# The low part of the MLP weights: an accumulating DMA in place of a subtraction on VectorE or GpSimd

## The chip, the cores and the metric

The kernel runs on one core of one Trainium2 chip. The metric is the device time of one execution in microseconds (us). In the profile PE is the tensor engine (PEld its weight loads), DVE is VectorE, ACT is ScalarE, POOL is GpSimd, and SP is the engine that only issues transfers.

## What is computed

One inference step of a two-layer decoder on 576 tokens (512 prompt tokens and 64 sample tokens). Each layer has a mixing part (retention, window attention, memory attention, gates, an output projection `w_out` and a LayerNorm) and an MLP part. The change touches the weights of the MLP alone:

```python
    x = layer_norm(ALPHA * x + merged @ w_out, ln1_g, ln1_b)
    h = jnp.square(jax.nn.relu(x @ w_up))                      # 1024 -> 4096
    return layer_norm(ALPHA * x + h @ w_down, ln2_g, ln2_b)    # 4096 -> 1024
```

All of it is float32. The kernel gets float32 accuracy out of the faster float32r matmul by keeping every operand in two parts: `hi`, the value rounded to float32r, and `lo`, what the rounding left (`lo = value - hi`). A product is then three matmuls into one PSUM bank: hi x hi, lo x hi, hi x lo.

## The kernel before

**Weights.** All projection weights are cut into units of 128 partitions x 1024 numbers (512 KB), 154 units a layer, in the order in which they are used. The last 64 units of a layer are the MLP's: four blocks `c`, each of 8 units of `w_up` (`("up", c, m)`) and 8 of `w_down` (`("dn", c, m)`). The eight units ahead of them are those of `w_out` (`("wo", m)`). For each unit `fetch()` has SP load the raw weights into a tile of the pool `A` (25 tiles), and `split()` makes `hi` and `lo` from it. In `split_into()` the rounding goes to ACT or DVE and the subtraction to DVE or POOL, whichever a clock kept while the program is written (`Clock`) takes to be free first (`soonest`, `rounded`, `pick`). Of the 128 MLP units, 75 are rounded on ACT and 53 on DVE; 120 are subtracted on DVE and 8 on POOL.

**Tokens.** They are two groups, A with 256 tokens and B with 320. One step (`mstep`) multiplies one unit with one group: 24 matmuls into one of three PSUM banks named `pg`, after which ACT or DVE evacuates the bank. A step needs a free bank, so it waits for the evacuation of three steps before.

**Order.** Normally a unit is used for A and then for B (`both`). Around the LayerNorms the order is skewed: the eight `wo` units run for A, then the same eight for B; then the eight `up` units of block 0 run for A, then for B; the last `dn` block is done like this too. So A's LayerNorm (`norm_ev`, generators `shift`, `half`, `last`) is worked off on DVE, ACT and POOL while PE does B's `wo` steps, and B's LayerNorm while PE does A's `up` steps. In these runs a new unit is due every A step, in the rest of the MLP every A and B step together.

**When a unit is split.** `tick()` runs after every few matmuls. It splits the next unit if that one is due within `LOOK` = 24 us of the plan, is no more than `cap` units ahead of the last one finished, and ACT is about to be idle (or it is due within 4 us). Instructions on an engine run in the order in which they were written, so a split that stands ahead of other work on ACT, DVE or POOL holds that work up.

The diff touches `split()` alone:

Of the kernel before, what the change touches and what calls it, by code (L numbers as in the profile page):

```python
# [11 lines left out]
AF = mybir.ActivationFunctionType  # L12
ALU = mybir.AluOpType
# [5 lines left out]
D = 1024  # L19
# [43 lines left out]
def unit_order():  # L63
    o = [("mk", m) for m in range(4)] + [("mv", i) for i in range(4)]
    for p in range(4):
        o += [("rk", p), ("rq", p), ("rv", p, 0), ("rv", p, 1), ("rg", 2 * p), ("rg", 2 * p + 1)]
    o += [("sv", 0), ("sk", 0)] + [("sq", m) for m in range(4)]
    for m in range(8):
        o += [("gr", m), ("br", m)]
    o += [("mq", m) for m in range(4)]  # L70
    for g, b in (("gs", "bs"), ("gm", "bm")):
        for i in range(4):
            o += [(g, 2 * i), (g, 2 * i + 1), (b, i)]
    o += [("wo", m) for m in range(8)]
    for c in range(4):
        o += [("up", c, m) for m in range(8)] + [("dn", c, m) for m in range(8)]
    return o
# [160 lines left out]


class Clock:  # L240
    """An estimate, kept while the program is written, of when each engine gets to an instruction. It only decides in
    which order independent work is put into the engines' queues."""
    HOP = 0.15

    def __init__(self):
# [98 lines left out]


class Pe(tuple):
    """What the tensor engine reads next, in a generator's yield."""


class Filler:  # L350
# [65 lines left out]
class Builder:  # L416
# [67 lines left out]
        return self.cst[:rows, a:b]  # L484

    def soonest(self, choices, *ins):
        """The engine of the (name, cost) pairs that is likely to end first with an operation on ins."""
        c = self.clock
        t = max([c.now] + [c.ready((i,)) for i in ins])
        return getattr(self.nc, min(choices, key=lambda x: max(c.te[x[0]], t) + x[1])[0])  # L490
# [18 lines left out]
    def fetch(self, u):  # L509
        self.raw[u] = self.tile([P, 8, P], tag="A")  # L510
        self.nc.sync.dma_start(self.raw[u], self.I["wall"][u])
        if u >= XFROM:
            next(self.between, lambda: None)()

    def split(self, u):
        raw = self.raw.pop(u)
        k = unit_order()[u % UNITS]
        if k[0] == "wo":
            b = True
        elif k[0] in ("up", "dn"):  # L520
            b = u % 2 == 0
        else:
            b = k[0] in ("gr", "br") and u % 4 == 0
        tl = "B" if b else "A"
        hi = self.tile([P, 8, P], F32R)
        lo = self.tile([P, 8, P], F32R, tag=tl)
        self.split_into(hi, lo, raw, True)
        self.w[u] = (hi, lo)

    def tick(self):  # L530
# [67 lines left out]
        return r  # L598

    def load_x(self, X):  # L600
        """The loads of x and of the constants, which fetch() starts between those of the first weights; yields then
        the splits of x."""
        sync = self.nc.sync
        raws = []

        def part(g, j):
            raw = self.tile([P, 4, NG[g]], tag=g)
            sync.dma_start(raw, self.I["xT"][:, 4 * j:4 * j + 4, OFF[g]:OFF[g] + NG[g]])
            raws.append((g, raw))

        def const(*names):
            for k in names:
                sync.dma_start(getattr(self, k), self.I[k])
        todo = [lambda: part("A", 0), lambda: part("A", 1), lambda: const("cst"), lambda: part("B", 0),
                lambda: part("B", 1), lambda: const("rope", "par")]

        def split():
            for i in range(4):
                while i >= len(raws):
                    yield 0.5  # L620
                g, raw = raws[i]
                yield (raw,)
                X.setdefault(g, {"h": [], "l": []})
                h = self.tile([P, 4, NG[g]], F32R, tag=g)
                lo = self.tile([P, 4, NG[g]], F32R, tag=g)
                self.split_into(h, lo, raw, True)
                X[g]["h"].append(h)
                X[g]["l"].append(lo)
        self.between = iter(todo)
        return split()  # L630

    def load_mem(self, M):
# [61 lines left out]
            V.scalar_tensor_tensor(out, a, 1.5, out, ALU.add, ALU.mult)  # L694

    def norm_ev(self, g, y, l, gi, eps, out, scale=None, bias=1.0):
        """Evacuation of the eight chunks of one token group that ends in LayerNorm. The sums of y - c and (y - c)^2
        grow chunk by chunk; c is the mean of the first two chunks, so that E[(y-c)^2] is at most four times the variance."""
        nc = self.nc
        V, S, T, G = nc.vector, nc.scalar, nc.tensor, nc.gpsimd  # L700
        n = NG[g]
# [3 lines left out]
            return self.par[:, l, gi + q:gi + q + 1], self.par[:, l, gi + 8 + q:gi + 9 + q]  # L705

        def mean(ps, src):
            """As a generator: the mean of src over the features. 1/D is exact in float32r, the two parts of src add up
            to src."""
            if out is None and g == "A":  # L710
                yield Pe((src,))
                T.matmul(ps, lhsT=self.ones.bitcast(F32), rhs=src, start=True, stop=True)
                return
            yield (src,)
            hi, lo = (self.tt()[:, :n].bitcast(F32R) for _ in range(2))
            self.split_into(hi, lo, src, True)
            yield Pe((lo,))
            for i, x in enumerate((hi, lo)):
                T.matmul(ps, lhsT=self.ones, rhs=x, start=(i == 0), stop=(i == 1))

        def shift():
            pm = self.bank("a")[:, :n]
            yield from mean(pm, st["acc"])
            yield (pm,)
            st["c"] = self.u(n)
            V.tensor_scalar(st["c"], pm, 4.0, None, ALU.mult)
            cb = st["c"].unsqueeze(1).to_broadcast([P, 4, n])
            self.pick(y[1], st["c"], bias=bias).tensor_tensor(y[1], y[1], cb, ALU.subtract)
# [12 lines left out]
        def last():  # L741
            p1, p2 = self.bank("a")[:, :n], self.bank("a")[:, :n]
            yield from mean(p1, st["acc"])
            yield from mean(p2, st["s2"])
            yield (p1,)
            t = self.tile([P, 320], tag="ln", bufs=2)[:, :n]
# [310 lines left out]
            yield Pe((t,))  # L1057

    def hi_lo(self, hi, lo, src):
        """As a generator: the two parts of src, in float32r."""  # L1060
        self.nc.scalar.copy(hi, src)
        yield (hi,)
        e = self.nc.vector if src.space == PSUM else self.pick(src, hi)
        e.tensor_tensor(lo, src, hi.bitcast(F32), ALU.subtract)
# [624 lines left out]
        return X2  # L1689

    def lazy(self, step, gen):
        """The step, once the generator gen() that computes its operand has run to its end."""
        def fn():
            self.fill.finish(gen())
            step[1]()
        return (step[0], fn, step[2])
# [76 lines left out]
```

## Time and profile before

| | before |
|---|---|
| time, median of 2 runs | 2206.39 us (2205.45 to 2207.34) |
| span of the profiled execution | 2203.7 us |
| PE busy | 2155.0 us (98%) |
| DVE busy | 1251.4 us (57%) |
| ACT busy | 678.1 us (31%) |
| POOL busy | 324.3 us (15%) |
| DMA, mean over the span | 99 GB/s |

Busy shares are means over stages with different limits. The stage in which an engine's time counts is the one in which another engine waits for it; the idle time in front of an instruction, and what ended it, show that. Almost all lines of code carry the number L331, since one helper records every operation, so instructions are told apart by the tiles they write and read (`B<-B,pg` writes a B tile and reads a B tile and a `pg` bank).

### The profile page before, as it was taken

Reading aid. Unit: us, or ns where it says so; the run is one execution under the profiler, and the core shown is the slowest. Engines: PE = TensorE matmul, PEld = TensorE weight load, DVE = VectorE, ACT = ScalarE, POOL = GpSimd, SP = SyncE. Lnnn points to the kernel's source line nnn. Section 1 sums busy time; section 2 is a strip of 40 time slices with the busy share of each in tenths; the row PEclk is TensorE's granted clock in tenths of the full one; section 3 lists DMA queues with packets and bytes.
Section 4 is the critical chain, followed back from the end, with each engine's and each line's share of the span. In section 5 each row is a group of like instructions: output and inputs, shape, how many; then the busy total and the mean of one; then the engine's idle time right before and its main releaser. Section 6 shows DMA issues by size and latency. Waiting matters only on the chain. (4 is left out here: it accounts for less than half of the span.)

```text
span 2203.7 us, 38686 instructions
## 1 busy us (share of the span) xinstructions
PE 2155.0 (98%) x16466; PEld 2095.4 (95%) x16466; DVE 1251.4 (57%) x2334; ACT 678.1 (31%) x1400; POOL 324.3 (15%) x283
## 2 busy tenths in 40 slices
PE   9999999999999999999999999999999999999996
PEld 8999999999998999999989998999999899999996
DVE  6666855456677434343876568554565864343346
ACT  3222234232135141405342221442321450504042
POOL 0222300011032000000432223000210420000003
PEclk9999999999999999999999999999999999999998
DMA  8222212333331222223252222122444222222211
GB/s 305 81 86 93 82 49 77 107 136 143 120 126 63 91 87 77 86 96 96 84 175 83 84 83 91 59 76 97 144 154 149 86 68 86 81 91 77 87 49 43
DMA packets 66732, 217.41 MB, mean 99 GB/s; under 512 B 7232, under 2 KB 16960, under 8 KB 66496
## 3 DMA queue, kind: packets, MB, share of 16 engines
q1 hardware_dynamic: 50944, 168.27, 22.8%
q0 software_dynamic: 10528, 38.80, 5.0%
q10 hardware_dynamic: 5088, 7.87, 1.1%
q8 instruction: 129, 2.11, 0.4%
q14 instruction: 43, 0.35, 0.1%
HBM read 200.89 MB, written 15.99 MB: 98 GB/s over the span
## 5 line engine op out<-in xcount | busy, mean ns | idle before, releaser
L331 PE MATMUL pg<-B,A 128*128 128x320 f32 x5920 | 1030.2, 311 | 13.5 <-DVE B L331 11.9
L331 PE MATMUL pg<-A,A 128*128 128x256 f32 (+1 forms) x6720 | 962.1, 286 | 12.5 <-DVE A L331 5.4
L331 PEld LDWEIGHTS pg<-B,A 128*128 128x128 f32 x5920 | 907.9, 189 | 20.1 <-DVE B L331 14.4
L331 PEld LDWEIGHTS pg<-A,A 128*128 128x128 f32 x6720 | 892.4, 192 | 29.2 <-issue 11.7
L331 DVE TENSOR_TENSOR A<-A,A 128x1024 fp32r<-128x1024 f32 (+4 forms) x234 | 270.0, 1161 | 65.3 <-ACT A L331 60.9
L331 ACT CAST A<-A 128x1024 fp32r<-128x1024 f32 (+4 forms) x263 | 238.0, 925 | 94.9 <-DVE A L331 73.1
L331 PE MATMUL pg<-A,B 128*128 128x256 f32 x1088 | 248.0, 283 | 0.0
L331 PE MATMUL pg<-B,B 128*128 128x320 f32 x704 | 219.4, 312 | 0.0
L331 ACT ACTIVATE u<-pg 128x320 f32<-128x320 f32 (+1 forms) x128 | 52.6, 411 | 477.0 <-PE pg L331 476.8
L331 POOL TENSOR_TENSOR A<-A,A 128x1024 fp32r<-128x1024 f32 (+2 forms) x43 | 92.8, 2162 | 679.5 <-ACT A L331 621.5
L331 PEld LDWEIGHTS pg<-A,B 128*128 128x128 f32 x1088 | 181.8, 192 | 0.0
L331 DVE TENSOR_TENSOR B<-u,B 128x320 fp32r<-128x320 f32 x80 | 39.3, 492 | 190.8 <-ACT B L331 190.8
L331 ACT ACTIVATE t<-pg 128x256 f32<-128x256 f32 (+1 forms) x128 | 52.6, 411 | 292.3 <-PE pg L331 292.1
L331 PEld LDWEIGHTS pg<-B,B 128*128 128x128 f32 x704 | 134.1, 191 | 0.0
L331 POOL TENSOR_TENSOR B<-A,A 128x1024 fp32r<-128x1024 f32 x13 | 35.4, 2720 | 555.1 <-ACT A L331 497.2
L331 DVE TENSOR_TENSOR B<-A,A 128x1024 fp32r<-128x1024 f32 x77 | 97.2, 1263 | 17.5 <-ACT A L331 16.2
L331 DVE CAST A<-A 128x1024 fp32r<-128x1024 f32 (+1 forms) x112 | 85.2, 760 | 7.4 <-DMA A<-d 7.3
L331 DVE TENSOR_TENSOR B<-B,pg 128x320 f32<-128x320 f32 x56 | 27.0, 484 | 106.8 <-PE pg L331 106.7
L331 DVE TENSOR_TENSOR B<-B,u 128x256 f32<-128x256 f32 (+3 forms) x84 | 74.5, 895 | 2.4
L331 POOL TENSOR_TENSOR A<-A,cst 128x512 fp32r<-128x512 f32 x32 | 43.7, 1394 | 152.7 <-ACT A L331 152.7
L331 DVE SCALAR_TENSOR_TENSOR B<-t,pg 128x320 f32<-128x320 f32 (+1 forms) x48 | 22.3, 464 | 72.0 <-ACT t L331 52.9
L331 DVE SCALAR_TENSOR_TENSOR u<-t,pg 128x256 f32<-128x256 f32 x64 | 28.8, 450 | 57.4 <-PE pg L331 57.3
(200 smaller groups left out, 1623.1 us busy)
## 6 DMA issues: line engine op xcount, KB each, us to landing
A<-in_wall SPq DMA_DIRECT2D x305, 512.0 KB, 3.3
A<-in_mck POOLq DMA_DIRECT2D x16, 512.0 KB, 4.2
A<-in_mcv POOLq DMA_DIRECT2D x16, 512.0 KB, 5.9
A<-in_s POOLq DMA_DIRECT2D x8, 512.0 KB, 4.4
out_state_s<-A POOLq DMA_DIRECT2D x8, 512.0 KB, 3.2
d<-A POOLq DMA_DIRECT2D x6, 512.0 KB, 7.7
A<-d ACTq DMA_DIRECT2D x6, 512.0 KB, 5.5
rc<-in_rc POOLq DMA_DIRECT2D x8, 256.0 KB, 3.0
```

Of the source, the lines that this page charges most:

```text
L331: r = f(*a, **kw)
```

## The change

For `up` and `dn` units the rounding goes to ACT always; ACT then writes the rounded weight with its sign turned into `lo` (a second pass over the raw weights, rounded in the same way), and a DMA issued by POOL adds the raw weights to it in SBUF. All other units, and all activations, are split as before. The diff also takes comments out, which changes nothing.

```diff
@@ def split(self, u):
         tl = "B" if b else "A"
         hi = self.tile([P, 8, P], F32R)
         lo = self.tile([P, 8, P], F32R, tag=tl)
-        self.split_into(hi, lo, raw, True)
+        if k[0] in ("up", "dn"):
+            self.nc.scalar.copy(hi, raw)
+            self.nc.scalar.activation(lo, raw, AF.Copy, scale=-1.0)
+            self.nc.gpsimd.dma_start(lo, raw, accum_op=ALU.add)
+        else:
+            self.split_into(hi, lo, raw, True)
         self.w[u] = (hi, lo)
```

Per MLP unit this leaves two ACT passes over 128x1024 and one 512 KB transfer from SBUF to SBUF on POOL's queue, in place of a rounding and a subtraction. The DMA waits for ACT's second pass; PE waits for the DMA; the tile of raw weights comes free when the DMA has landed.

The order of instructions shifts at two places. The first is on DVE, in the eight `wo` steps for group B, while A's LayerNorm is worked off. `B919` and `B920` are the two halves of B's accumulated row `y`, `pg` the banks that PE waits for, `par` the LayerNorm's gains, `A917` and `A918` A's `y`. Before, from the evacuation of the fourth B step to that of the fifth:

```order
L331 TENSOR_TENSOR A1017_7219<-A1005_7152,A1016_7218 128x1024
L331 SCALAR_TENSOR_TENSOR B919_6560<-B919_6560,pg1013_7188 128x320
L331 TENSOR_SCALAR A917_6556<-A917_6556,par8_85 128x256 x2
L331 TENSOR_TENSOR A1003_7145<-A917_6556,A1001_7143 128x512
L331 TENSOR_SCALAR A917_6556<-A917_6556,par8_85 128x256 x2
L331 TENSOR_TENSOR A1003_7145<-A917_6556,A1001_7143 128x512
L331 TENSOR_SCALAR A918_6557<-A918_6557,par8_85 128x256 x2
L331 TENSOR_TENSOR A1004_7146<-A918_6557,A1002_7144 128x512
L331 TENSOR_SCALAR A918_6557<-A918_6557,par8_85 128x256 x2
L331 TENSOR_TENSOR A1004_7146<-A918_6557,A1002_7144 128x512
L331 TENSOR_TENSOR B920_6561<-B920_6561,pg1018_7240 128x320
```

With the change, the same stretch:

```order
L331 SCALAR_TENSOR_TENSOR B919_6560<-B919_6560,pg1013_7191 128x320
L331 TENSOR_SCALAR A917_6556<-A917_6556,par8_85 128x256 x2
L331 TENSOR_TENSOR A1001_7138<-A917_6556,A999_7136 128x512
L331 TENSOR_SCALAR A917_6556<-A917_6556,par8_85 128x256 x2
L331 TENSOR_TENSOR A1001_7138<-A917_6556,A999_7136 128x512
L331 TENSOR_TENSOR B920_6561<-B920_6561,pg1018_7244 128x320
```

The subtraction of a weight (first row of before) is gone, and the evacuation of the fifth step stands behind two of the four pairs that finish A's LayerNorm, no longer behind all four.

The second place is on ACT, in the `up` steps of block 0 for group A. `u` rows are the evacuations of a step (squared ReLU and its rounding), `ln` rows belong to B's LayerNorm. Before:

```order
L331 CAST A1053_7479<-A1019_7259 128x1024
L331 CAST A1056_7491<-A1045_7435 128x1024
L331 ACTIVATE u1058_7501<-pg1051_7463 128x256
L331 ACTIVATE u1058_7501<-u1058_7501 128x256
L331 CAST A1032_7380<-u1058_7501 128x256
L331 ACTIVATE ln1059_7507<-pa1030_7378 128x320
L331 ACTIVATE ln1063_7525<-u1061_7522 128x320
L331 ACTIVATE ln1063_7525<-ln1063_7525 128x320
L331 ACTIVATE u1064_7542<-pg1060_7509 128x256
```

With the change, from the same evacuation of the third step on:

```order
L331 ACTIVATE u1056_7506<-pg1052_7470 128x256
L331 ACTIVATE u1056_7506<-u1056_7506 128x256
L331 CAST A1032_7385<-u1056_7506 128x256
L331 ACTIVATE ln1059_7513<-u1057_7510 128x320
L331 ACTIVATE ln1059_7513<-ln1059_7513 128x320
L331 CAST A1067_7552<-A1043_7416 128x1024
L331 ACTIVATE A1068_7553<-A1043_7416 128x1024
L331 ACTIVATE u1069_7563<-pg1060_7517 128x256
```

The rounding of the last of the eight `up` units (`A1056` before, `A1067` with the change) stood ahead of the third evacuation; it now stands behind it and behind the two `ln` rows, with the new negating pass at its heels.

## Rows read from the trace of the kernel before

**Rows 1.** Page, part 1: busy time, share of the span, instructions.

```profile
PE 2155.0 (98%) x16466; PEld 2095.4 (95%) x16466; DVE 1251.4 (57%) x2334; ACT 678.1 (31%) x1400; POOL 324.3 (15%) x283
```

**Rows 2.** Stretches: us, busy of PE, PEld, DVE, ACT, POOL, clock, DMA share, GB/s.

```profile
660.00:680.00 20.00, 14.49 (x81) 13.96 (x82) 18.84 (x27) 5.93 (x11) 9.92 (x8) 0.83 0.16 54
680.00:700.00 20.00, 20.00 (x168) 20.00 (x167) 16.79 (x22) 15.29 (x33) 4.98 (x7) 1.00 0.09 27
740.00:1040.00 300.00, 300.00 (x2252) 300.00 (x2251) 112.97 (x163) 83.51 (x167) 0.00 (x0) 1.00 0.26 85
...
1750.00:1770.00 20.00, 14.44 (x81) 13.66 (x80) 18.83 (x28) 7.91 (x14) 8.43 (x7) 0.84 0.21 73
```

**Rows 3.** Timeline of PE: start us, length us, what, [idle before <- releaser].

```profile
660.67 0.41 PE L331 MATMUL pg<-B,A 128*128 128x320 f32 x1 [0.67 <-DVE B L331]
673.09 0.63 PE L331 MATMUL pg<-B,A 128*128 128x320 f32 x1 [4.74 <-DVE B L331]
...
1765.43 0.64 PE L331 MATMUL pg<-B,A 128*128 128x320 f32 x1 [4.77 <-DVE B L331]
```

**Rows 4.** Timeline of PEld: the 24 weight loads of one undisturbed B step.

```profile
843.08 3.54 PEld L331 LDWEIGHTS pg<-B,A 128*128 128x128 f32 x24
```

**Rows 5.** Timeline of DVE in layer 0's `wo` steps for B.

```profile
645.96 0.69 DVE L331 CAST A<-A 128x1024 fp32r<-128x1024 f32 x1
646.68 1.22 DVE L331 TENSOR_TENSOR B<-A,A 128x1024 fp32r<-128x1024 f32 x1
...
650.21 2.65 DVE L331 TENSOR_TENSOR ln<-ln 128x256 f32<-128x256 f32 x1
...
653.91 2.52 DVE L331 SCALAR_TENSOR_TENSOR u<-ln,ln 128x256 f32<-128x256 f32 x1
...
662.89 1.21 DVE L331 TENSOR_TENSOR A<-A,A 128x1024 fp32r<-128x1024 f32 x1
...
665.75 2.77 DVE L331 TENSOR_TENSOR A<-A,A 128x512 fp32r<-128x512 f32 x1
668.45 0.72 DVE L331 TENSOR_SCALAR A<-A,par 128x256 f32<-128x256 f32 x2
669.20 0.69 DVE L331 TENSOR_TENSOR A<-A,A 128x512 fp32r<-128x512 f32 x1
...
672.56 0.48 DVE L331 TENSOR_TENSOR B<-B,pg 128x320 f32<-128x320 f32 x1
```

**Rows 6.** Timeline of POOL in the same stretch: subtractions for weights.

```profile
650.16 2.42 POOL L331 TENSOR_TENSOR A<-A,A 128x1024 fp32r<-128x1024 f32 x1 [4.76 <-ACT A L331]
...
653.55 2.59 POOL L331 TENSOR_TENSOR B<-A,A 128x1024 fp32r<-128x1024 f32 x1
...
665.52 2.45 POOL L331 TENSOR_TENSOR B<-A,A 128x1024 fp32r<-128x1024 f32 x1
```

**Rows 7.** Groups by shape, 740 to 1040 us: busy us, mean ns, idle before.

```profile
L331 DVE TENSOR_TENSOR A<-A,A 128x1024 fp32r<-128x1024 f32 x24 | 29.4, 1226 | 6.0 <-ACT A L331 5.6
L331 DVE TENSOR_TENSOR B<-A,A 128x1024 fp32r<-128x1024 f32 x23 | 28.2, 1226 | 5.5 <-ACT A L331 5.1
L331 ACT CAST A<-A 128x1024 fp32r<-128x1024 f32 x23 | 24.1, 1049 | 0.0
L331 DVE TENSOR_TENSOR A<-u,A 128x256 fp32r<-128x256 f32 x24 | 10.2, 425 | 16.8 <-ACT A L331 16.8
```

**Rows 8.** Page, parts 3 and 6: POOL's queue q0; KB, us from issue to landing.

```profile
q0 software_dynamic: 10528, 38.80, 5.0%
...
A<-in_wall SPq DMA_DIRECT2D x305, 512.0 KB, 3.3
A<-in_mck POOLq DMA_DIRECT2D x16, 512.0 KB, 4.2
...
d<-A POOLq DMA_DIRECT2D x6, 512.0 KB, 7.7
```

**Rows 9.** Timeline of POOL around 1093 us: two issues of 512 KB each.

```profile
1093.42 1.60 POOL L331 DMA_DIRECT2D d<-A  x2
```

**Rows 10.** Groups by shape on POOL, whole span: an issue of 512 KB.

```profile
L331 POOL DMA_DIRECT2D A<-in_mck x16 | 8.7, 546 | 133.4 <-PE pg L331 105.7 <-DVE A L331 26.1 <-PE pa L331 1.6
```

**Rows 11.** Timeline of ACT and PE at the end of A's `up` steps.

```profile
690.80 0.47 ACT L331 ACTIVATE ln<-ln 128x320 f32<-128x320 f32 x1
...
699.56 3.16 PE L331 MATMUL pg<-A,A 128*128 128x256 f32 x25
```

More of the change, by code (lines that the diff above doesn't have):

```diff
@@ L346 @@
 class Pe(tuple):
+    pass
 class Filler:
```

## The prediction

> **What bounds the kernel now.** I read the busy times first, then the stretches, then the waits in the few stretches that are not full. PE is busy for 2155.0 of 2203.7 us [rows 1], so 48.7 us of idle time is all that could come back at PE's present pace. The stretches say where: from 740 to 1040 us, which is the MLP's blocks after the first `up` run, PE is busy for 300.00 of 300.00 us at full clock while DVE works for 113 us, ACT for 84 and POOL not at all [rows 2]. The work that the change takes from DVE there keeps nobody waiting. The stretch 660 to 680 us is different: PE is busy for 14.49 us of 20, its granted clock is 0.83 of full on the mean, and DVE works for 18.84 us [rows 2]. That is where B's `wo` steps run over A's LayerNorm. PE idles for 4.74 us until DVE has evacuated a bank, and for 0.67 us a little ahead of that [rows 3]; layer 1 shows the same hole, 4.77 us [rows 3], 0.84 of the clock and 81 matmuls in both [rows 2]. So DVE sets the time there, and MLP weights are split on it in that very stretch.
>
> **What the hole costs.** An undisturbed B step issues 24 matmuls in 3.54 us [rows 4], 0.1475 us each. The 81 matmuls of the 20 us [rows 2] should take 11.9 us; 8.1 us are lost, some 5.5 of them idle and the rest at the lower clock that follows the idling. Layer 1 loses as much: 16.2 us in all.
>
> **Does the change close it?** The evacuation that ends the hole starts at 672.56 us [rows 5]. Ahead of it in DVE's queue since 645.96 us stand a rounding and two subtractions for MLP weights, 0.69, 1.22 and 1.21 us [rows 5], together 3.1, which go. Three LayerNorm operations there run several times longer than their like: 2.65 and 2.52 us for 128x256, which elsewhere takes 0.425 us [rows 5, 7], and 2.77 us for a shape that takes 0.69 a little later [rows 5]. Each starts within half a microsecond of a POOL subtraction of 2.4 to 2.6 us for a weight [rows 6]. I read that as the two engines holding each other up; with the POOL subtractions gone, 2.2 + 2.1 + 2.1 = 6.4 us go. Last, the order shows two pairs of 0.72 + 0.69 us [rows 5] moved behind the evacuation: 2.8 us. Together the evacuation comes 12.3 us earlier, where 4.74 + 0.67 = 5.4 us are needed.
>
> Against that stands new work on ACT, which A's LayerNorm also passes through. In this stretch four units are split: four negating passes and one rounding that DVE did, at 1.05 us each for 128x1024 [rows 7] (the negating pass is in no row; it has the same engine and shape, so I take the same time), 5.25 us. Even if all of it delays the chain, 12.3 - 5.25 = 7.0 us are left, more than 5.4. I take the hole as closed: -16.2 us. The bounds are 0 (ACT in its place) and -16.2.
>
> **ACT in A's `up` run.** From 680 to 700 us ACT is busy for 15.29 us [rows 2]; it evacuates every step and works on B's LayerNorm. Three more units are split there, which adds 3.15 us of negating passes. The 4.7 idle microseconds could hold them, but each pass that stands ahead of an evacuation makes it late, and a step needs the bank of three steps before. Between 0 and 3.15 us I take 1.5 in each layer: +3.
>
> **The wait for the last `up` unit.** A's `up` run needs a new unit every A step, so here the DMA's latency is least covered. The rounding of the eighth unit now stands on ACT behind the LayerNorm's exponential, which ends at 690.80 + 0.47 = 691.3 us [rows 11]. Two passes of 1.05 us [rows 7] end at 693.4, POOL's issue of 0.55 us [rows 10] at 693.9. PE begins that unit's step at 699.56 us [rows 11] (on the scale of before; both shift together). The DMA may thus take 5.6 us. No row shows an accumulating DMA or one from SBUF to SBUF. A 512 KB transfer takes 3.3 us from issue to landing on SP's queue, and on POOL's 4.2 us as a load and 7.7 us as a store [rows 8]. The accumulate reads two streams. From POOL's queue, 5.0% of 16 engines over 2203.7 us by 10528 packets is 0.167 us a packet of about 4 KB [rows 8]; 128 rows of 4 KB on 16 engines make 8 x 0.167 = 1.34 us for one pass. I take the load on the same queue and one more pass, 4.2 + 1.34 = 5.5 us, so the unit arrives just in time: 0. The bounds are 3.3 us (also 0) and twice the slowest, 15.4 us, which is a rival below.
>
> A DMA's issue is itself not always 0.55 us: two stores took 1.60 us together [rows 9], 0.25 us more each, worth about 0.1 us here. The Trainium skill (SBUF — State Buffer, "SBUF: two separate sides" and the section after it) speaks against the change at this point: POOL writes the descriptors of its DMAs through a port pair that DVE shares, is locked out while DVE runs a copy or tensor_scalar in a two-port mode, and a 620 ns DMA was seen to take 3100 ns. By that rule the unit would be up to 2.5 us late in each layer and the sum below 5 us higher; by the row 0.2. I go by the row.
>
> **The steady MLP.** From 740 to 1040 us 47 units were split (24 + 23 subtractions [rows 7]), one in 6.38 us. ACT gets 47 negating passes and the 24 roundings that it did not do, 75 us on top of 83.5 [rows 2] in 300: it stays half idle. POOL gets one issue of 0.55 us per unit and had nothing to do there [rows 2]; nothing that PE needs is queued behind it. The plan splits a unit up to 24 us ahead, against 2.1 + 0.55 + 5.5 = 8.2 us: hidden. If that cover is gone, the rate decides. The DMA engines are 26% busy with 47 loads in 300 us [rows 2], 1.66 us a unit, which leaves 6.38 - 1.66 = 4.72 us for the accumulate. Two passes are 2.7 us: it fits. The lower bound is one pass, 1.34 us; the upper one the whole 7.7 us of the slow store [rows 8] as engine time, which does not fit.
>
> **The sum.** 2203.7 - 16.2 + 3 + 0 = 2190.5 us for the profiled execution. The median of before lies 2.7 us above its profile, so 2193 us.
>
> **The rivals.**
> - *The accumulate is too slow for the pace* (the one on the slow side). It decides once a DMA takes more than 4.72 us of all 16 engines, 0.59 us per 4 KB row, 3.5 times a plain packet. PE then waits in every unit. At four passes, 5.34 us, a unit takes 0.62 us more, 128 units 80 us: 2273 us; at the upper bound, 7.7 us, 2.98 x 128 = 381 us: 2574. For it: nothing measured excludes it. Against it: two reads and a write explain two passes, not four.
> - *The rate suffices but the landing is long.* At 15.4 us the last `up` unit lands at 693.9 + 15.4 = 709.3, 9.8 us late. The last `dn` block has the same run of A steps; priced alike, four such places give 39 us: 2232. For it: one store in the trace already takes 7.7 us. Against it: the loads on the same queue land in 4.2.
> - *ACT takes DVE's place in A's LayerNorm*, the hole stays, and only the cost is left: 2206.4 + 3 = 2209 us. For it: 5.25 us of new work in the chain. Against it: 12.3 us go from the same chain, and ACT is busy for only 5.93 of the 20 us of the hole [rows 2].
> - *More than 2% faster* needs 44 of the 48.7 us of PE's idle time; most of it lies in places without MLP weights.
>
> **How the numbers follow.** Forecast, hidden and the hole closed: 0.60, with a range of its own from 2183 (with the negating passes free and a few microseconds besides) to 2203. Too slow for the pace: 0.19. Long landing: 0.10. ACT in DVE's place: 0.10. Over 2% faster: 0.01. The predicted time is that of the first. The range runs from 2182 to 2240, which holds the first, third and fourth and leaves out 0.20. Two per cent, 44 us, is about what a measurement of this kernel can tell from no change. Faster 0.01, slower 0.19, within 0.80.
>
> **What the profile after would show.** Right: no wait of PE for a B evacuation in the `wo` steps, some 130 matmuls at full clock in the 20 us that held 81; DVE's 128x256 LayerNorm operations back at 0.42 us; 300 of 300 us of PE in the middle of the MLP, with DMAs of 512 KB on POOL's queue landing in about 5.5 us. Wrong: PE or its weight loads waiting for a DMA into a `lo` tile; landings that grow from unit to unit and a DMA share near 1.0, which is the rate; waits at the eighth `up` unit alone, which is the latency; or an ACT row in front of the LayerNorm where DVE stood. I would be most wrong if the accumulate takes its two streams much slower than two plain packets.

## The result and the profile after

The changed kernel takes 2187.1 us (median of 2 runs, 2185.9 to 2188.4) where the kernel before takes 2206.4: a ratio of 0.9916 (95% interval 0.9887 to 0.9945), 19 us less, which by the bound of 2% is "within". The forecast was 2193 us. The span of the profiled execution went from 2203.7 to 2184.1 us.

The page of the kernel after, part 1 (busy time, share of the span, instructions), beside [rows 1]:

```profile
PE 2147.9 (98%) x16466; PEld 2089.6 (96%) x16466; DVE 1060.2 (49%) x2164; ACT 846.9 (39%) x1581; POOL 411.2 (19%) x400
```

DVE lost 191 us of work, ACT got 169 and POOL 87. PE's own busy time fell by 7 us although it does the same matmuls: fewer of them run at the lower clock (on the mean 0.83 and 0.84 of full in the two `wo` stretches of before, 1.00 now). The stretches of the kernel after (us, busy of PE, PEld, DVE, ACT, POOL, clock, DMA share, GB/s), beside [rows 2]:

```profile
660.00:680.00 20.00, 20.00 (x154) 20.00 (x153) 14.46 (x27) 12.27 (x22) 9.85 (x10) 1.00 0.44 107
740.00:1040.00 300.00, 300.00 (x2255) 300.00 (x2254) 43.93 (x97) 148.74 (x237) 40.56 (x48) 1.00 0.70 171
1100.00:1120.00 20.00, 15.58 (x89) 13.98 (x89) 19.80 (x23) 12.88 (x22) 9.92 (x8) 0.91 0.45 152
1750.00:1770.00 20.00, 20.00 (x162) 20.00 (x161) 14.49 (x23) 16.96 (x31) 10.53 (x11) 1.00 0.57 122
```

The hole of the `wo` steps is gone in both layers: PE works 20.00 of 20 us at full clock, with 154 and 162 matmuls where 81 stood. The steady MLP was full and is full, although the DMA engines are busy 0.70 of the time there instead of 0.26. The third row is a place that the diff does not touch, B's LayerNorm at the end of layer 0; PE still has a hole there, and one of the experiments below comes back to it.

DVE's timeline in the `wo` steps for B, beside [rows 5]:

```profile
649.41 0.42 DVE L331 TENSOR_TENSOR ln<-ln 128x256 f32<-128x256 f32 x1
...
650.32 0.42 DVE L331 SCALAR_TENSOR_TENSOR u<-ln,ln 128x256 f32<-128x256 f32 x1
...
662.14 0.48 DVE L331 TENSOR_TENSOR B<-B,pg 128x320 f32<-128x320 f32 x1
```

The LayerNorm operations that took 2.65 and 2.52 us are back at 0.42, and the evacuation that PE waited for starts at 662.14 instead of 672.56.

The new transfers, in parts 3 and 6 of the page (POOL's queue q0 with packets, MB, share of 16 engines; then the tile written and read, the queue, KB, us from issue to landing), beside [rows 8]:

```profile
q0 software_dynamic: 28960, 105.92, 22.0%
...
B<-A POOLq DMA_DIRECT2D x64, 512.0 KB, 5.2
A<-A POOLq DMA_DIRECT2D x64, 512.0 KB, 5.3
```

The queue carries 18432 packets more, 144 for each of the 128 accumulates, and 17.0% more of 16 engines over 2184 us: 0.322 us a packet on the mean, 2.9 us of all engines for each accumulate. The steady MLP gives about the same: (0.70 - 0.26) x 300 us over 47 units is 2.8 us. The time to landing is counted from the start of the issue, so the issue is part of it. Their issue on POOL and the negating pass on ACT, by shape from 740 to 1040 us (busy us, mean ns, idle before and its releasers), beside [rows 7, 10]:

```profile
L331 ACT ACTIVATE A<-A 128x1024 fp32r<-128x1024 f32 x23 | 24.3, 1055 | 19.9 <-DMA B<-A 19.9
...
L331 POOL DMA_DIRECT2D A<-A x23 | 19.8, 859 | 151.2 <-ACT u L331 78.4 <-ACT A L331 61.2 <-PE pg L331 11.6
```

The pass costs what a rounding costs. The issue takes 0.86 us, 0.31 more than that of a plain 512 KB transfer.

### The profile page after: what moved, and what is told of

Same layout as the page of the kernel before. It is cut to its first block, busy times and chain, and to the rows that moved or that the text cites. A ratio compares the mean times of both kernels' runs of the same rounds, so it can differ in the third digit from the quotient of the medians.

```text
span 2184.1 us, 39229 instructions
## 1 busy us (share of the span) xinstructions
PE 2147.9 (98%) x16466; PEld 2089.6 (96%) x16466; DVE 1060.2 (49%) x2164; ACT 846.9 (39%) x1581; POOL 411.2 (19%) x400
## 3 DMA queue, kind: packets, MB, share of 16 engines
q8 instruction: 129, 2.11, 0.4%
## 5 line engine op out<-in xcount | busy, mean ns | idle before, releaser
L331 ACT CAST A<-A 128x1024 fp32r<-128x1024 f32 (+4 forms) x316 | 294.0, 943 | 208.1 <-DVE A L331 73.1
L331 DVE TENSOR_TENSOR A<-A,A 128x1024 fp32r<-128x1024 f32 (+3 forms) x173 | 191.1, 1115 | 49.6 <-ACT A L331 46.2
L331 POOL TENSOR_TENSOR A<-A,A 128x1024 fp32r<-128x1024 f32 (+2 forms) x40 | 84.5, 2117 | 331.7 <-ACT A L331 273.6
L331 POOL DMA_DIRECT2D A<-A x64 | 55.7, 870 | 354.5 <-ACT u L331 177.1
L331 POOL DMA_DIRECT2D B<-A x64 | 55.0, 860 | 260.2 <-ACT B L331 115.8
L331 DVE TENSOR_TENSOR A<-u,A 128x256 fp32r<-128x256 f32 x72 | 30.5, 423 | 136.8 <-ACT A L331 129.0
L331 ACT ACTIVATE A<-A 128x1024 fp32r<-128x1024 f32 (+1 forms) x70 | 73.9, 1055 | 52.6 <-DMA B<-A 34.9
L331 ACT ACTIVATE B<-A 128x1024 fp32r<-128x1024 f32 x64 | 67.4, 1053 | 0.0
```

What stands on the lines that cost most here:

```text
L331: r = f(*a, **kw)
```

## Experiments

The theory after the result: the whole gain comes from the eight `up` units of block 0 in each layer, which are split while A's LayerNorm is worked off; there the change takes work from DVE's queue and, more than that, the POOL subtractions that hold DVE up. The other 112 of the 128 units neither gain nor lose, as long as the DMA is covered, that is, has landed before PE asks for the unit. Three groups of runs test where the gain is, what holds DVE up, and where the cover ends. The runs were made on three chips, and each is compared with the kernel before on its own chip (medians 2209.2, 2209.7 and 2206.1 us), so across the runs it is the ratios that are compared.

### Where the gain is

**The DMA for block 0's `up` units alone, and for all but these.**

```diff
-        if k[0] in ("up", "dn"):
+        if k[:2] == ("up", 0):
```

> The DMA makes the low part only for the eight up units of block 0 in each layer (16 of 128 units); the other 112 are split as before. Theory (the gain is the closed hole in A's LayerNorm after w_out, where only these units are split): all of the gain, 2187 us, between 2185 and 2191, and no PE wait for a B evacuation in the wo steps. Rival (the gain comes from relieving DVE and POOL all over the MLP): at most 16/128 of it, 2204 us. Rival (half from each LayerNorm of a layer): about 2197 us.

Measured 2188.2 us, ratio 0.9915 (0.990 to 0.993): all of the gain from 16 units. The stretch of the `wo` steps is full here too:

```profile
660.00:680.00 20.00, 20.00 (x147) 20.00 (x146) 16.39 (x27) 11.09 (x18) 10.31 (x11) 1.00 0.48 125
```

```diff
-        if k[0] in ("up", "dn"):
+        if k[0] in ("up", "dn") and k[:2] != ("up", 0):
```

> The other half: the DMA for 112 of 128 units, not for the up units of block 0. Theory: no gain and no loss, 2206 us, between 2203 and 2209, with the 4.7 us wait of PE still there. Rival (relief all over): 2189 us. If the DMAs of the steady MLP cost anything that the hole's gain hid, it shows here as more than 2209 us.

Measured 2206.8 us, ratio 0.9989 (0.9979 to 0.9999), a tenth of a per cent. PE's timeline in this kernel (start, length, what, [idle before <- releaser]) shows the hole of [rows 3] unchanged, 4.77 and 4.74 us:

```profile
672.23 0.64 PE L331 MATMUL pg<-B,A 128*128 128x320 f32 x1 [4.77 <-DVE B L331]
...
1764.15 0.43 PE L331 MATMUL pg<-B,A 128*128 128x320 f32 x1 [4.74 <-DVE B L331]
```

What follows: 112 accumulates of 512 KB cost nothing, and bring no more than this tenth of a per cent, of which 1.8 us in the profiled run lie behind the last matmuls (the last paragraph on why the prediction was right comes back to them). The place is shown.

### What held DVE up

**No DMA, every MLP weight subtracted on DVE and none on POOL.** This takes the neighbour away and gives DVE more work than before: in A's LayerNorm five subtractions of 1.22 us instead of two and a rounding of 0.69, which goes to ACT.

```diff
-            self.nc.scalar.activation(lo, raw, AF.Copy, scale=-1.0)
-            self.nc.gpsimd.dma_start(lo, raw, accum_op=ALU.add)
+            self.nc.vector.tensor_tensor(lo, raw, hi.bitcast(F32), ALU.subtract)
```

> No DMA: all 128 units are rounded on ACT and subtracted on DVE, none on POOL. It parts the two causes that the prediction added up: operations taken from DVE (3.1 us) and the lengthening of DVE's LayerNorm operations beside POOL's subtractions (6.4 us). If the lengthening is real, taking POOL's three subtractions out gives 6.4 us and putting them on DVE costs 3 x 1.22 = 3.7 us, less the 0.69 us of a rounding: a net 3.4 us, so PE's 5.4 us of idle time shrink to about 2 and the time is about 2198 us, between 2193 and 2203. Rival (only DVE's own work counts, the long rows are an artefact): DVE has 3 us more to do ahead of the evacuation, PE idles for about 8 us, 2212 us or more.

Measured 2201.6 us, ratio 0.997 (0.9959 to 0.9982). DVE's two LayerNorm rows of 2.65 and 2.52 us take 0.42 and 0.99 here (the second beside a POOL operation of 0.97 us that is no subtraction for a weight), and PE's hole in layer 0 is 2.98 us instead of 4.74:

```profile
653.02 0.42 DVE L331 TENSOR_TENSOR ln<-ln 128x256 f32<-128x256 f32 x1
...
653.93 0.99 DVE L331 SCALAR_TENSOR_TENSOR u<-ln,ln 128x256 f32<-128x256 f32 x1
```
```profile
672.92 0.64 PE L331 MATMUL pg<-B,A 128*128 128x320 f32 x1 [2.98 <-DVE B L331]
```

**No DMA, block 0's `up` units all subtracted on POOL and none on DVE**, the counterpart; the other units as before.

```diff
-        if k[0] in ("up", "dn"):
+        if k[:2] == ("up", 0):
             self.nc.scalar.copy(hi, raw)
-            self.nc.scalar.activation(lo, raw, AF.Copy, scale=-1.0)
-            self.nc.gpsimd.dma_start(lo, raw, accum_op=ALU.add)
+            self.nc.gpsimd.tensor_tensor(lo, raw, hi.bitcast(F32), ALU.subtract)
```

> No DMA. Everything is as before, but the eight up units of block 0 in each layer are rounded on ACT and subtracted on POOL, none on DVE: the counterpart to the run in which DVE subtracted them all and POOL none. It frees DVE of its 3.1 us of rounding and subtractions in A's LayerNorm and leaves it the lengthening. Theory: POOL's subtractions of 2.4 us lengthen the DVE operations beside them, three of the five or so here falling into LayerNorm operations; the gain of 3.1 us is spent on that, the hole of PE stays at 3 to 5 us a layer: 2206 us (2200 to 2211), slower than with all of them on DVE (2201.6). DVE rows of 128x256 of over 2 us are again seen. Rival: only DVE's own queue counts and POOL's subtractions are free: the hole closes as far as with the DMA, 2190 us (2186 to 2196).

Measured 2215.4 us, ratio 1.0023 (1.0013 to 1.0032): a little slower than the kernel before, and 4 us above my range, 3 of which are the chip's (2209.7 us for the kernel before). Relieving DVE of its own work there makes the time longer. PE's hole grows from 4.74 to 5.67 us:

```profile
673.21 0.64 PE L331 MATMUL pg<-B,A 128*128 128x320 f32 x1 [5.67 <-DVE B L331]
```

A second loss, which I had not counted, arises right behind, in B's LayerNorm. The timelines of POOL and of DVE there:

```profile
682.21 2.40 POOL L331 TENSOR_TENSOR A<-A,A 128x1024 fp32r<-128x1024 f32 x1
684.57 2.63 POOL L331 TENSOR_TENSOR B<-A,A 128x1024 fp32r<-128x1024 f32 x1
687.16 2.65 POOL L331 TENSOR_TENSOR A<-A,A 128x1024 fp32r<-128x1024 f32 x1
```
```profile
682.28 2.68 DVE L331 TENSOR_TENSOR rc<-rc,u 128x320 f32<-128x320 f32 x1 [1.72 <-POOL rc L331]
684.88 2.68 DVE L331 TENSOR_TENSOR t<-accB,t 128x320 fp32r<-128x320 f32 x1
687.48 2.61 DVE L331 TENSOR_TENSOR A<-u,A 128x256 fp32r<-128x256 f32 x1
```

Three POOL subtractions stand back to back, and with each there is one small DVE operation (some 0.4 to 0.5 us elsewhere) that starts just after it and ends 0.3 us after it: 684.96 against 684.61, 687.56 against 687.20, 690.09 against 689.81. The rows of before fit the same pattern [rows 5, 6]: 652.86 against 652.58, 656.43 against 656.14, and 668.52 against 667.97 for the operation of 0.69 us. DVE does not run slower beside POOL; it looks like waiting until POOL's instruction is over and then doing its own. This is how the Trainium skill tells it (SBUF — State Buffer, "SBUF: two separate sides"): the pair of ports that the two share is "an **exclusive lock**, not a bandwidth split", held for a whole instruction by whoever starts first, also against a DVE operation with two SBUF inputs. By that rule and by these rows alike, a small DVE operation costs up to the length of POOL's instruction on top of its own.

Rows a little earlier in the same kernel show two more sides of it, DVE and then POOL:

```profile
660.61 1.94 DVE L331 TENSOR_TENSOR B<-B,u 128x1280 f32<-128x1280 f32 x1
662.48 0.47 DVE L331 SCALAR_TENSOR_TENSOR B<-B,pg 128x320 f32<-128x320 f32 x1
663.06 2.11 DVE L331 TENSOR_TENSOR accB<-accB,B 128x320 f32<-128x320 f32 x1
```
```profile
661.16 3.66 POOL L331 TENSOR_TENSOR A<-A,A 128x1024 fp32r<-128x1024 f32 x1
```

POOL's subtraction takes 3.66 us instead of some 2.4: it starts within a DVE operation that ends at 662.55, and ends 2.27 us after that, so POOL can be the one that waits. And the evacuation at 662.48, which reads a `pg` bank in PSUM besides one tile in SBUF, takes its usual 0.47 us in the midst of this subtraction, while the operation behind it, on tiles in SBUF alone, takes 2.11. So POOL does not hold up the evacuation itself, but the LayerNorm operations that stand ahead of it in DVE's queue.

**The changed kernel, and layer 1's first 16 units subtracted on DVE alone.** The same cause in a place that the change did not touch, the third row of the stretches after. In the changed kernel, DVE, POOL and the wait of PE:

```profile
1099.52 2.71 DVE L331 SCALAR_TENSOR_TENSOR u<-ln,ln 128x320 f32<-128x320 f32 x1
1102.26 3.63 DVE L331 TENSOR_TENSOR B<-B,u 128x640 f32<-128x640 f32 x2
...
1108.80 3.37 DVE L331 TENSOR_TENSOR A<-A,A 128x1024 fp32r<-128x1024 f32 x1
```
```profile
1099.46 5.01 POOL L331 TENSOR_TENSOR A<-A,A 128x1024 fp32r<-128x1024 f32 x2 [4.58 <-ACT A L331]
1108.50 2.59 POOL L331 TENSOR_TENSOR A<-A,A 128x1024 fp32r<-128x1024 f32 x1 [4.03 <-ACT A L331]
```
```profile
1112.23 1.44 PE L331 MATMUL pg<-A,A 128*128 128x256 f32 x5 [4.42 <-DVE A L331]
```

The edit:

```diff
+        elif UNITS <= u < UNITS + 16:
+            self.rounded(hi, raw)
+            self.nc.vector.tensor_tensor(lo, raw, hi.bitcast(F32), ALU.subtract)
         else:
             self.split_into(hi, lo, raw, True)
```

> The changed kernel, and in addition the first 16 units of layer 1's projections, which are split while layer 0's last LayerNorm of group B is worked off, are subtracted on DVE always, none on POOL. In the changed kernel PE still waits there 4.42 us for a DVE subtraction, and that one takes 3.37 us beside a POOL subtraction; two LayerNorm operations ahead of it take 2.71 and 3.63 us where 1.0 and 1.6 are usual. Theory: the two engines' subtractions lengthen each other here as in the LayerNorm that the change mended. Without POOL's, DVE gets three subtractions of 1.22 us more and loses some 5.9 us of lengthening; the unit that PE waits for is ready about 3.4 us earlier, of which group B's LayerNorm, by then about 1 us late, lets 2.5 count. Against the changed kernel on the same chip: 2.5 us faster (1 to 5), PE's wait of 4.42 us down to about 1 to 2. Rival: DVE's queue is simply too long there, its three subtractions more cost what they save: the same within 1 us or slower by up to 3, the wait stays over 4 us.

and beside it the changed kernel again:

> The changed kernel once more, unaltered, beside the run that moves the next layer's subtractions to DVE, so that the two are compared on one chip. Expected: 0.9915 of the kernel before (0.990 to 0.993), all that the DMA in block 0 alone gave. Rival: the two runs of the first comparison overstated it, and it is 0.994 or more.

Measured 2183.9 us (four runs, 2182.8 to 2184.0), ratio 0.9899 (0.9883 to 0.9916), against 2187.9 (four runs, 2185.7 to 2188.6), ratio 0.9917 (0.9902 to 0.9932), for the changed kernel: 4 us by the medians, whose runs do not overlap, 2.0 us by the profiled spans (2181.9 and 2183.9). The second run confirms the first result. DVE's timeline, PE's and the stretch in the kernel with the edit:

```profile
1102.01 0.49 DVE L331 SCALAR_TENSOR_TENSOR u<-ln,ln 128x320 f32<-128x320 f32 x1
1102.54 1.56 DVE L331 TENSOR_TENSOR B<-B,u 128x640 f32<-128x640 f32 x2
...
1107.01 4.62 DVE L331 TENSOR_TENSOR A<-A,A 128x1024 fp32r<-128x1024 f32 x4
```
```profile
1093.58 0.86 PE L331 MATMUL pg<-A,A 128*128 128x256 f32 x5 [3.32 <-DVE A L331]
...
1108.28 3.50 PE L331 MATMUL pg<-A,A 128*128 128x512 f32 x17 [1.18 <-DVE A L331]
```
```profile
1100.00:1120.00 20.00, 18.82 (x116) 16.80 (x115) 19.69 (x34) 14.26 (x24) 3.40 (x6) 1.00 0.61 212
```

The long rows are gone, as expected: 0.49 and 1.56 us, and four subtractions at 1.16 us each. The wait of 4.42 us falls to 1.18. A part of it came back earlier, 3.32 us at 1093.58, where the subtractions that POOL used to do now hold up a unit on DVE; I had not forecast that one. The next B step begins at 1117.5 us instead of 1120.2. This kernel beats both the kernel before and the changed one, by a little.

### Where the cover ends

**The DMA for the `wo` units too**, which are wanted one per A step, with a short lead.

```diff
-        if k[0] in ("up", "dn"):
+        if k[0] in ("wo", "up", "dn"):
```

> The low parts of the eight w_out units of each layer are made by the accumulating DMA as well. They are wanted in A's wo steps, a new unit every A step. My theory: what decides is the lead, the time from ACT's rounding to PE's use. In the changed kernel a unit needs two ACT passes of 1.05 us, an issue of 0.86 us and a landing of 5.2 us, 8.2 us in all; as the program emits them, the last four w_out units have 4 to 7 us. I expect waits of PE or its weight loads for a DMA in A's wo steps, some 4 us a layer and as much again by the lower clock after the idling at most: 2199 us (2192 to 2210). Rival: the program's emission times are too pessimistic, the DMA is hidden here too, and the time stays at 2187 (2185 to 2190) or a little below, since still more leaves DVE.

Measured 2200.7 us, ratio 0.995 (0.9933 to 0.9968): 8 us of the gain are lost again. The waits are where they were expected, 3.7 us in layer 0 and 4.2 in layer 1, on PE's timeline, with the DMA's issue on POOL's below:

```profile
631.55 0.39 PE L331 MATMUL pg<-A,B 128*128 128x256 f32 x1 [3.29 <-DMA B<-A]
```
```profile
626.86 0.86 POOL L331 DMA_DIRECT2D B<-A  x1 [7.95 <-ACT B L331]
```

The matmul starts 4.7 us after the start of the issue, which itself stood directly behind ACT's negating pass. Since a landing counts from the start of the issue, a unit needs the two passes and a landing, 2.1 + 5.2 = 7.3 us; the 8.2 of the expectation counts the issue twice. So the latency, not the rate, ends the cover first.

**The rounding back on DVE, the DMA kept.**

```diff
-            self.nc.scalar.copy(hi, raw)
+            self.nc.vector.tensor_copy(hi, raw)
```

> The DMA stays, but the rounding of the up and dn weights goes back from ACT to DVE; ACT keeps the negating pass. Theory: ACT's second pass costs nothing in the changed kernel (B's up run starts as much earlier as A's), so nothing is to be won on ACT; and DVE gets 0.69 us a unit back just where its queue is long, in A's LayerNorm and in A's up run, so the last units of block 0 are split later: the program emits them with 0 to 2 us of lead, against the 8.2 us that two passes, issue and landing take. I expect PE to wait for the last one or two up units, up to 8 us a layer: about 2205 us (2190 to 2212). Rival: ACT's passes do cost something, and the time falls to 2184 (2181 to 2187). A reading by the way: POOL's issue of the DMA takes 0.86 us in the changed kernel; if a DVE rounding of 128x1024 holds POOL up, issues that begin during one take 1.2 us or more.

Measured 2206.0 us, ratio 0.9983 (0.9973 to 0.9992): nearly the whole gain is lost, though most of the hole in layer 0 stays closed (from A's LayerNorm statistics to A's `up` run 26.69 us, against 25.40 in the kernel after and 33.94 before). The last `up` unit of block 0 is rounded behind B's LayerNorm on DVE at 691.28, and PE waits for its DMA, 4.41 us in layer 0 and 4.29 in layer 1; the clock is 0.87 on the mean from 680 to 700 us, where it was full in the kernel after:

```profile
692.29 0.86 POOL L331 DMA_DIRECT2D A<-A  x1 [3.90 <-ACT u L331]
```
```profile
696.88 5.13 PE L331 MATMUL pg<-A,A 128*128 128x256 f32 x23 [4.41 <-DMA A<-A]
```

What follows: that both passes of a unit go to ACT is no detail of the change. ACT is the engine that is early enough there; the same DMA behind a late rounding is worth almost nothing. The reading by the way stays undecided: 43 of the 45 issues from 740 to 1040 us take 0.85 to 0.89 us, and the other two, 1.16 and 1.10, overlap a rounding on DVE but also follow closely on each other, and the second of two in a row takes 1.20 elsewhere too. Outside that stretch issues that overlap a rounding take from 0.86 (at 1830.05 and 2132.86) to 1.40 us (at 736.39). The issue at 692.29 follows a rounding and takes 0.86.

**Two accumulates for each unit.** The low part comes out with double weight here.

```diff
-            self.nc.scalar.activation(lo, raw, AF.Copy, scale=-1.0)
+            self.nc.scalar.activation(lo, raw, AF.Copy, scale=-2.0)
+            self.nc.gpsimd.dma_start(lo, raw, accum_op=ALU.add)
             self.nc.gpsimd.dma_start(lo, raw, accum_op=ALU.add)
```

> The accumulate is issued twice for each of the 128 units, onto minus twice the rounded weight, so the low part comes out doubled. It asks where the rate begins to bind. From the profile after, the DMA engines are 70% busy from 740 to 1040 us against 26% before, so one accumulate takes 0.44 x 300/47 = 2.8 us of all 16 engines, and a load 1.66. Two accumulates make 5.6 + 1.66 = 7.3 us a unit against PE's 6.38. Theory: rate-bound, 0.9 us a unit and 128 units: 115 us more than after, about 2300 us (2270 to 2350), with the DMA share near 1.0 and PE waiting for DMAs. Rival (the engines' busy share overstates what they need, there is room): 2187 to 2200 us.

Measured 2487.5 us (one run), far over the expected 2300, and not for the reason I had: this run does not test the rate. Its timeline of POOL:

```profile
801.69 0.86 POOL L331 DMA_DIRECT2D A<-A  x1 [5.64 <-DMA A<-A]
802.23 1.21 POOL L331 DMA_DIRECT2D B<-A  x1
809.42 0.86 POOL L331 DMA_DIRECT2D B<-A  x1 [5.98 <-DMA B<-A]
```

The second accumulate writes the tile that the first one writes, so its issue waits on POOL until the first has landed, and the next unit's first accumulate stands behind it in POOL's queue. A unit takes the first accumulate's landing and the 0.54 us between two issues, 7.7 us here (801.69 to 809.42), where the pace is 6.38. POOL waits 742 us in all for its own DMAs, while the engines are not full (DMA share 0.88 in the steady MLP). The second of two issues that start some 0.5 us apart takes 1.21 us here.

**Two plain stores more for each unit**, which depend on nothing but the raw weights, put the question of the rate again. Their tensors in DRAM are read by nobody.

```diff
             self.nc.gpsimd.dma_start(lo, raw, accum_op=ALU.add)
+            for _ in range(2):
+                self.nc.gpsimd.dma_start(self.dram([P, 8, P]), raw)
```

> The changed kernel, and POOL stores the raw weights of each MLP unit twice more, to two scratch tensors in DRAM that nobody reads (work added, nothing of the result). Unlike a second accumulate, these DMAs wait for nothing. This asks for the rate at which the steady MLP breaks. A unit has 6.38 us; the changed kernel uses 0.70 of it, 4.5 us. Two more passes of 512 KB at 1.34 us each or more make 7.2 us. Theory: the 16 engines are then full, the DMA share in the steady MLP goes to 1.0, landings grow, and PE waits some 0.8 us in every unit: 2285 us (2250 to 2320). Rival: there is more room than the share says, and the time stays under 2200 us.

Measured 2260.4 us (one run). The steady MLP, and the landings:

```profile
740.00:1040.00 300.00, 297.81 (x2218) 297.24 (x2218) 41.75 (x92) 140.97 (x219) 89.76 (x139) 0.99 1.04 324
```
```profile
B<-A POOLq DMA_DIRECT2D x64, 512.0 KB, 13.5
A<-A POOLq DMA_DIRECT2D x64, 512.0 KB, 14.1
```

The engines are full, and the landing has grown from 5.2 to about 14 us, as the theory said; but PE idles for only 2.2 of 300 us in the steady MLP and does 2218 matmuls where it did 2255, 1.6% fewer. The stores do wait after all: POOL idles for 147 us over the whole run in front of them until an earlier DMA has landed, and why is not shown. The time is lost where the lead is short, in A's `up` run (waits of 3.13, 4.03 and 4.15 us from 690 to 710 us) and in the last `dn` block. With 45 accumulates at 2.8 us, 45 loads at 1.66 and 92 stores in 312 us of engine time (1.04 x 300), a store takes 1.2 us, not the 1.34 that I had assumed. This is an estimate, which takes the other two as in the kernel after; by it a unit needs 2.8 + 1.66 + 2.4 = 6.9 us where it has 6.38. So the rate seems to end close to where it was counted, and what is missing is taken from the lead first: the sign of it is again the latency.

## Why the prediction was right

The likeliest case came true, with all its signs, some 6 us below the forecast. By its own steps, with the same PE rows as marks (anchors) in both traces:

- **The hole.** Forecast -8.1 us a layer. From the start of A's LayerNorm statistics to the start of A's `up` run, the kernel after needs 8.54 us less in layer 0, and by the next anchors 8.54 less in layer 1. Right in place, cause and size. The evacuation comes 10.4 us earlier, 9.7 of them within the stretch; forecast were 12.3, less at most 5.25 for ACT. What is missing was not lost on ACT, for which DVE does not wait there: DVE waits 1.45 us for PE at the start (before 646.79), and a pair of 128x512 operations at 650.78 takes 2.49 us instead of 1.29, beside a POOL operation of 1.22 us that the change left there. The 81 matmuls of the 20 us were to become some 130; they became 154, because A's `up` steps, which are shorter, now fall into the window.
- **POOL and DVE holding each other up** was read from rows of before alone. The runs show it: without POOL's subtractions the long rows go even when DVE gets more work (0.997), with more of them the kernel gets slower than before (1.0023). How much of the 8.5 us is this and how much DVE's own 3.1 us can be told roughly: taking the neighbour away gave back 3.9 us in layer 0, by the distance of the same anchors, while DVE took on 3.0 us more, so that the neighbour is worth some 6.9 us as an estimate (forecast 6.4).
- **ACT in A's `up` run.** Forecast +1.5 us a layer, measured 0: B's `up` run begins 9.25 us earlier than before, as A's does. This is the term that was mis-sized. I let the passes stand in front of evacuations; they fell into ACT's idle time: in the same 20 us of the program (from 670.75 us in the kernel after) ACT is busy for 18.45 us instead of 15.29, as forecast, and PE does 168 matmuls in both.
- **The last `up` unit.** Forecast in time with a landing of 5.5 us; it is issued at 683.45 and, at the median of 5.3, lands at 688.8; PE takes it up at 690.31. The issue takes 0.86 instead of 0.55 us, too little to matter, and it is part of the landing, so that the prediction's sum (693.4 + 0.55 + 5.5) counted it twice, on the safe side. The 2.5 us of lateness that the prediction named beside its own row did not come; no VectorE copy runs beside this issue, so the run does not test the rule behind them. The margin is about 1.5 us: in the run with the rounding on DVE this very unit is late.
- **The steady MLP.** Forecast an accumulate of 2.7 us of 16 engines and no effect; measured 2.8 to 2.9 and none (300.00 of 300.00). The estimate of two plain passes held, a little by luck: an accumulate has 144 packets and not the 128 that I counted for a pass, and with 144 two plain passes come to 3.0 us. The accumulate takes 0.322 us a packet where a plain one took 0.167 [rows 8].
- **The rivals.** The pace is kept with 1.9 us a unit to spare, so the slow case did not come; it needs two more stores a unit to show. Landings stayed at 5.2. ACT did not take DVE's place in A's LayerNorm.

Of the 17.4 us by which PE's last anchor comes earlier (2141.58 before, 2124.16 after), 17.1 are the two holes; 0.7 us come ahead of the first anchor, and 0.4 are given back between. The end of the span is 19.6 us earlier, so 2.2 us more are gained after the last matmuls. The 2.2 are not part of the mechanism that was forecast. They come in all nine kernels here that have accumulating DMAs, whether 16 or 256 of them: from the start of the last matmul to the end of the span these take 13.6 to 14.2 us, the three without (before, all on DVE, block 0 on POOL) 15.8 or 15.9. What causes it stays open, and the 0.7 are not explained by a run either. The 6 us by which the forecast was too high are the 3 us for ACT, these 2.2, and about 1 from the holes and the 0.7.

## What to carry to other kernels

Look for the stretch in which PE waits, not at the busiest engine: 112 of the 128 moved subtractions were worth next to nothing, 16 were worth all of it, and ACT's second pass was free because ACT idled just there. Work on GpSimd beside a short VectorE operation on the path whose inputs lie in SBUF can cost that operation the whole length of GpSimd's instruction, so moving the subtraction to either of the two engines is not symmetrical, and a small operation with several times its usual length is the sign to look for. A DMA in place of an engine's pass is covered as long as its chain (here two passes and a landing that includes the issue, 7.3 us) is shorter than the lead with which the data are made; count that lead at the point where it is shortest.

## What the runs showed of the hardware

- Issuing an accumulating DMA of 512 KB from SBUF to SBUF takes POOL 0.86 us, a plain load 0.546 [rows 10]; the second of two that start some 0.6 us apart takes 1.20 to 1.22.
- Such a DMA lands 5.2 us after the start of its issue (median) and takes 2.8 to 2.9 us of the 16 engines: 144 packets of 3.6 KB on the mean, 0.322 us each.
- A DVE operation on SBUF tiles that starts just after a POOL subtraction of 128x1024 ends somewhat less than its own length after POOL's: 0.3 us after for those of 0.4 to 0.5 us, 1.1 us after for a subtraction of 1.2 (1108.80 + 3.37 against 1108.50 + 2.59). An evacuation that reads a PSUM bank and one SBUF tile kept its 0.47 us beside such a subtraction (at 662.48), and a POOL subtraction that started within a DVE operation took 3.66 us (at 661.16).
- With the DMA share at 1.04, landings went from 5.2 to 14 us while PE did 1.6% fewer matmuls in 300 us.
- In the run with the rounding on DVE, landings into B tiles rose to 6.4 us while those into A tiles stayed at 5.2. This was not followed up.
